# Hybrid decoder layer with a mixture of experts: pair 14's rows sent through memory, the residual rows loaded between the sent rows, two shared-row products moved

## The chip, the cores and the metric

The kernel runs on one core of one Trainium2 chip. The metric is the device time of one execution in microseconds, as the median of several runs; lower is better. Engines are named as in the profile: PE is TensorE, DVE VectorE, ACT ScalarE, POOL GpSimd, SP the SyncE that issues most DMAs.

## The reference

One decoder layer over 512 tokens of width 1024 (16 learned meta tokens in front). First a mixer (latent attention heads beside short convolutions), which ends in a residual sum `h`. Then the part that matters here:

```python
h = h + rms_norm(mix, post_mix_norm[l])
ffn = hier_moe(rms_norm(h, pre_ffn_norm[l]), ...)
h = h + rms_norm(ffn, post_ffn_norm[l])
```

`hier_moe` routes each token to one of 4 groups and to the best 2 of the group's 8 experts (32 experts in all, width 256), and adds one shared expert that every token goes through:

```python
hid = jax.nn.silu(a) * b * combine[:, :, None]
routed = jnp.einsum('nef,efd->nd', hid, w_down)
shared = (jax.nn.silu(t @ w_sh_gate) * (t @ w_sh_up)) @ w_sh_down
return (routed + shared).reshape(bsz, slen, d)
```

All data is float32.

## The kernel before, in words

The program is written out instruction by instruction. Generators (`pairs_gen`, `last_gen`, `shared_gen` and others) are spawned with priorities, and `run` picks at build time the one that can go on first by a model of the engines' progress; the order that results is fixed in the program. A `yield` names what the generator waits for in that model.

The 32 experts are taken as 16 pairs, j = 0 to 15 (`pairs`, line 393). An expert holds up to 64 tokens in the main path; a pair fills the 128 rows of a tile. For each pair `pairs_gen` (line 1452) does this: the pair's tokens are gathered from `t_d` in memory into `xg` by an indirect transfer on GpSimd, transposed into `wk` (`pxt`), multiplied with the two gate-and-up blocks of each expert (`pgu`, blocks `(e, 0)` and `(e, 1)`, 1 MB each), gated (`hidden`, ScalarE and VectorE), transposed again (`pht`), and multiplied with the down block `(e, 2)` in two halves (`pdn`).

What becomes of a pair's rows depends on `PE_PAIRS` (line 56), here 2, so `first` is 14. Pairs 0 to 13 copy the down product into `yb` (one half by ScalarE, one by VectorE) and `send` it: an indirect transfer on GpSimd writes each row to its place in `y_d`, whose 1024 rows hold two rows for each token. Pairs 14 and 15 go through TensorE: `y_out` splits the down product into a rounded part and a rest in `ys`, a selection matrix `sel` is built from the token numbers, and sel times `ys` puts the rows at their tokens. For pair 14 this is `combine`: sixteen products `pcb` between the two gate-and-up halves of pair 15, each pair of them added by VectorE to the shared expert's rows `sho` (`acc(c)`, four chunks of 128 tokens).

For pair 15 `last_gen` (line 1531) takes over. For each chunk c it collects two banks `pca` on TensorE: the shared rows times the identity (`inject`), `ys` times `sel`, and the sum of the two sent rows of each token times the identity (`ld kk`, loaded from `y_d` and added by VectorE in `rows`). Then ScalarE squares the banks for the norm, VectorE multiplies them by the gain (`tm`), GpSimd takes the power (`rf`), and `store` adds the residual `h` (`ld hb`, loaded from `h_d`) and issues the output. Before, chunks 0 and 1 are injected ahead of the last down product, chunks 2 and 3 in their turn. A last copy by ScalarE puts `pca` back into `acc(c)`, for the case that some expert holds more than 64 tokens: then a branch at the end (`overflow`) handles the rest. With these inputs the trace shows no work in that branch.

The weights and the last loads stand in one list, `Slots.queue`, in the order of the `queue_load` calls (lines 379 to 406). They go into 25 buffers of 1 MB each and are issued in that order on SP's queue. A DMA on SP waits for the semaphore of the DMA eight places ahead of it, and a `kk` load also for the sends into `y_d`. An instruction that waits on SP holds everything behind it.

Of the kernel before, what the change touches and what calls it, by code (L numbers as in the profile page):

```python
# [18 lines left out]
P = 128  # L19
D = 1024  # L20
NT = 4
# [31 lines left out]
LAT_TO_PE = 0.2  # L53
GROUPS = ((0, 2), (2, 4))
POOL_M = 4
PE_PAIRS = 2

# [106 lines left out]
def hymba_kernel(ctx: ExitStack, tc: tile.TileContext, xT, xmT, x, meta, cpk, pos, wqkv, wconv, wuq, wukv,  # L166
# [120 lines left out]
    def at(*aps):  # L287
        return lambda: max(PR.when(a) for a in aps)

    def free_bank(n=1):  # L290
        def f():
            if len(banks) + n <= NBANK:
                return 0.0
            return sorted(done(b) for b in banks)[len(banks) + n - NBANK - 1]
        return f
# [7 lines left out]
    def flag(d, *names):  # L303
        return lambda: 0.0 if all(n in d for n in names) else INF
# [4 lines left out]
    def every(*needs):  # L309
        return lambda: max(f() for f in needs)  # L310
# [64 lines left out]
    def queue_load(name, src, n=2048, ok=None):  # L375

        Slots.queue.append((name, src, n, ok))
# [22 lines left out]
        if j == S_AT:  # L400
            queue_load((NE, 2), we[NE, 2])
    queue_load("gp", g_post[None, :].to_broadcast([P, D]), D)
    for q in range(2):
        queue_load(f"hb{q}", h_d[q * 256:(q + 1) * 256, :].rearrange("(q p) d -> p q d", p=P))
    for c in range(NT):
        queue_load(f"kk{c}", y_d[:, :].rearrange("(k c p) d -> c p k d", k=2, c=NT)[c], ok=lambda: "sent" in cv)


    jp = m1.bitcast(I32)[:, 0:P]
# [973 lines left out]
    def overflow():  # L1383

        n = nc.values_load(ov["novf"][0:1, 0:1], min_val=0, max_val=16)  # L1385
        with tc.If(n > 0):
            with tc.For_i(0, n, 1) as i:
                overflow_tile(i)
            post_again()
# [62 lines left out]
    def pairs_gen():  # L1452
        wk_, yb, ys, box = rt["wk"], rt["yb"], None, None
        rt["jk"] = wk_.bitcast(BF)[:, 3584:3584 + 512]
        xt_ = wk_[:, :D]
        sg, hd, ht = (wk_[:, D + q * 256:D + (q + 1) * 256] for q in range(3))
        yield every(at(xg[0]), free_bank(2))
        xpose(xg[0], xt_)
        gather(2)
        first = NP - PE_PAIRS  # L1460
        for j, es in enumerate(pairs):
            ps = None
            for i in range(2):
                yield every(loaded(*((e, i) for e in es)), free_bank())
                w = [got((e, i)) for e in es]
                yield at(*w, xt_)
                if ps is None:
                    ps = bank("pgu")
                for k in range(4):
                    col2(ps, xt_[:, (4 * i + k) * P:(4 * i + k + 1) * P],  # L1470
                         [w[q][:, k * 512:(k + 1) * 512] for q in range(2)], i + k == 0, i + k == 4)
                rel(*w)
                if j > first and i == 0:
                    yield flag(sh, "done")
                    for half in range(2):
                        for c in range(NT):
                            yield every(at(ys), free_bank())
                            combine(ys, sel, HALF[half], c)
            hidden(ps, wgt[:, j:j + 1], sg, hd)
            sh["silu"] = True  # L1480
            if j == S_GO:
                sh["go"] = True
            if j == first:
                box = reserve("ys", dt=F32R)
                rel(yb)
                yield lambda: 0.0 if box else INF
                rt["ys"] = ys = box[0]
            if j + 1 < NP:
                yield every(at(xg[(j + 1) % 2]), free_bank(2))
                xpose(xg[(j + 1) % 2], xt_, V)  # L1490
            if j + 3 < NP:
                gather(j + 3)
            yield every(at(hd), free_bank())
            hidden_t(hd, ht)
            if j >= first:
                V.tensor_tensor(sel.rearrange("p (c n) -> p c n", c=NT), iop[:, None, :].to_broadcast([P, NT, P]),
                                tok[:, :, j:j + 1].to_broadcast([P, NT, P]), op=OP.is_equal)
            if j == NP - 1:
                spawn(last_gen(es), 5)
                return  # L1500
            yield every(loaded(*((e, 2) for e in es)), free_bank(2))
            w = [got((e, 2)) for e in es]
            yield at(*w, ht)
            for half in range(2):
                ps = down(half, ht, [t[:, half * D:(half + 1) * D] for t in w])
                if j >= first:
                    y_out(ps, ys, HALF[half])
                else:
                    o = yb[:, j % 2 * D:(j % 2 + 1) * D][:, HALF[half]]
                    if half:  # L1510
                        V.tensor_copy(o, ps)
                    else:
                        S.activation(o, ps, AF.Copy)
            rel(*w)
            if j < first:
                send(j, yb[:, j % 2 * D:(j % 2 + 1) * D])
            if j == first - 1:
                cv["sent"] = True
# [6 lines left out]
    def down(half, ht, w):  # L1525
# [2 lines left out]
            col2(ps, ht[:, f * P:(f + 1) * P], [w[q][:, f * 512:(f + 1) * 512] for q in range(2)], f == 0, f == 1)  # L1528
        return ps

    def last_gen(es):


        ys, ht = rt["ys"], rt["wk"][:, D + 512:D + 768]
        ss, rf = small([P, 2 * NT], "ssf"), small([P, NT], "rf")
        var = small([P, 2 * NT], "var")
        pa, kk = {}, {}

        def inject(c):

            for half in range(2):
                pa[c, half] = bank("pca")
                held.append(pa[c, half])
                mm(pa[c, half], ident, acc(c)[:, HALF[half]], start=True, stop=False)

        for c in range(2):
            yield every(flag(sh, "done"), at(acc(c)), free_bank(2))
            inject(c)
        yield every(loaded(*((e, 2) for e in es)), free_bank(2))
        w = [got((e, 2)) for e in es]  # L1550
        yield at(*w, ht)
        for half in range(2):
            y_out(down(half, ht, [t[:, half * D:(half + 1) * D] for t in w]), ys, HALF[half])
        rel(*w)
        tm = reserve("tm0", "tm1")
        yield every(loaded("gp", "hb0", "hb1"), lambda: 0.0 if len(tm) == 2 else INF)
        gp, hb = got("gp"), [got("hb0"), got("hb1")]
        fin.update(gp=gp, tm=tm)

        def rows(c):  # L1560

            kk[c] = got(f"kk{c}")
            V.tensor_tensor(kk[c][:, :D], kk[c][:, :D], kk[c][:, D:2 * D], op=OP.add)

        def tmc(c, o=slice(0, D)):
            return tm[c // 2][:, c % 2 * D:(c % 2 + 1) * D][:, o]

        def store(c):
            h = hb[c // 2][:, c % 2 * D:(c % 2 + 1) * D]
            for q in HALF:  # L1570
                V.scalar_tensor_tensor(h[:, q], tmc(c, q), rf[:, c:c + 1], h[:, q], op0=OP.mult, op1=OP.add)
                Y.dma_start(out[c * P:(c + 1) * P, q], h[:, q])

        yield loaded("kk0")
        rows(0)
        for c in range(NT):
            if c >= 2:
                yield free_bank(2)
                inject(c)
            yield at(ys)  # L1580
            for half in range(2):
                for q in range(2):
                    mm(pa[c, half], sel[:, c * P:(c + 1) * P], ys[:, q * D + half * 512:q * D + (half + 1) * 512],
                       start=False, stop=False)
            yield at(kk[c])
            for half in range(2):
                mm(pa[c, half], ident, kk[c][:, HALF[half]], start=False, stop=True)
            if c + 1 < NT:
                yield loaded(f"kk{c + 1}")
                rows(c + 1)  # L1590
            for half in range(2):
                S.activation(rt["jk"], pa[c, half], AF.Square, accum_out=ss[:, 2 * c + half:2 * c + half + 1])
                V.tensor_tensor(tmc(c, HALF[half]), pa[c, half], gp[:, HALF[half]], op=OP.mult)
            v = var[:, 2 * c:2 * c + 2]
            V.tensor_scalar(v[:, 0:1], ss[:, 2 * c:2 * c + 1], 1.0 / D, EPS, op0=OP.mult, op1=OP.add)
            V.scalar_tensor_tensor(v[:, 1:2], ss[:, 2 * c + 1:2 * c + 2], 1.0 / D, v[:, 0:1], op0=OP.mult, op1=OP.add)
            G.tensor_tensor(rf[:, c:c + 1], v[:, 1:2], neghalf[:, 0:1], op=OP.pow)
            for half in range(2):
                S.activation(acc(c)[:, HALF[half]], pa[c, half], AF.Copy)
                held.remove(pa[c, half])  # L1600
            if c:
                store(c - 1)
        store(NT - 1)

# [93 lines left out]
```

## Time and profile before

| | |
|---|---|
| median of 3 runs | 516.67 us (515.33 to 517.06) |
| the profiled execution | 516.31 us |
| its span, first to last instruction | 514.5 us |
| busy in the span: PE, DVE, ACT, POOL | 95%, 45%, 33%, 17% |
| moved by DMA | 151.07 MB, mean 294 GB/s |
| mean granted TensorE clock | 0.994 |

The page gives shares over the whole span. The change lies in the last 50 us or so, so the views of that stretch, engine by engine, say more: the instructions in order of time, the windows of 2 us, and the DMA issues with their time from issue to landing. A row of the order of time gives start, duration, engine, line, operation, tiles, how many, and in brackets the idle time before it and what ended it. A landing is the time at which the transfer's semaphore came, counted from its issue. Most instructions have line 314 or 159, those of two helpers; they are told apart by their tiles.

### The profile page before, as it was taken

The page shows a single profiled execution, that of the slowest core. Times are in us where ns is not written, and L with a number is a line of the kernel's source. Part 1 is how long each engine was busy: PE and PEld are TensorE (multiplying, and loading weights), DVE is VectorE, ACT ScalarE, POOL GpSimd, SP SyncE. Part 2 cuts the span into 40 slices and gives each one's busy share as a digit, 9 for nine tenths or more (in the row PEclk, how much of TensorE's full clock was granted, in tenths as well). Part 3 has the DMA queues.
Part 4 walks back from the last instruction along what each step waited for, and adds up shares of the span by engine and source line. Part 5 has one row for each costly group of instructions (what it writes and reads, how often), then busy time and mean ns, then how long its engine had stood idle before and what let it go on. Part 6 is the DMA issues. An engine that isn't in the chain of part 4 may idle for free. (4 is left out here: it accounts for less than half of the span.)

```text
span 514.5 us, 7298 instructions
## 1 busy us (share of the span) xinstructions
PE 487.5 (95%) x2782; PEld 306.5 (60%) x2782; DVE 232.9 (45%) x532; ACT 168.9 (33%) x343; POOL 88.0 (17%) x113
## 2 busy tenths in 40 slices
PE   7999999999999999999999999999999998889992
PEld 7998999788767788898844333433333332323341
DVE  6467789657878633588821200111111111003384
ACT  5775526444444642441211221211111111101152
POOL 2034234400000003540201110111111110000011
PEclk9999999999999999999999999999999999999997
DMA  8952240190208578499289999999999999999953
GB/s 288 400 236 82 83 164 0 46 365 0 83 25 300 211 304 329 172 384 395 88 347 392 425 420 421 422 418 422 417 421 418 420 419 419 423 420 421 408 214 125
DMA packets 30165, 151.07 MB, mean 294 GB/s; under 512 B 5392, under 2 KB 5776, under 8 KB 16048
## 3 DMA queue, kind: packets, MB, share of 16 engines
q1 hardware_dynamic: 24512, 138.43, 67.0%
q0 software_dynamic: 4320, 7.94, 4.2%
q10 hardware_dynamic: 1296, 4.21, 2.0%
q8 instruction: 23, 0.38, 0.3%
q14 instruction: 14, 0.11, 0.1%
HBM read 140.54 MB, written 17.83 MB: 308 GB/s over the span
## 5 line engine op out<-in xcount | busy, mean ns | idle before, releaser
L314 PE MATMUL pc<-xh,cw 128*128 128x256 f32 (+2 forms) x320 | 70.0, 309 | 0.0
L159 DVE SCALAR_TENSOR_TENSOR wk<-wk,wgt,pgu 128x256 f32<-128x256 f32 x16 | 7.7, 480 | 110.3 <-ACT wk L159 110.3
L314 PEld LDWEIGHTS pc<-xh,cw 128*128 128x128 f32 x320 | 52.3, 189 | 4.0 <-issue 1.3
L159 ACT ACTIVATE wk<-pgu 128x256 f32<-128x256 f32 x16 | 6.2, 384 | 142.0 <-PE pgu L314 142.0
L314 PE MATMUL pc<-xl,cw 128*128 128x256 f32 (+2 forms) x160 | 48.8, 305 | 0.0
L159 POOL DMA_INDIRECT xg<-t_d,idx x16 | 17.0, 1065 | 113.8 <-PE pxt L314 69.2
L159 DVE COPY yb<-pdn 128x512 f32<-128x512 f32 x14 | 9.7, 692 | 55.4 <-PE pdn L314 55.4
L314 PEld LDWEIGHTS pc<-xl,cw 128*128 128x128 f32 x160 | 30.3, 189 | 1.2
L159 POOL DMA_INDIRECT y_d<-yb,sidx x14 | 14.1, 1010 | 81.1 <-DVE yb L159 60.2
L159 ACT ACTIVATE att<-pS,nm 128x128 f32<-128x128 f32 (+3 forms) x32 | 16.9, 528 | 29.3 <-DVE nm L159 27.2
L314 PE MATMUL pS<-kT,qT 128*128 128x128 f32 (+3 forms) x64 | 22.7, 440 | 0.0
L159 POOL TENSOR_TENSOR sst<-rst,neghalf 128x1 f32<-128x1 f32 x12 | 7.6, 635 | 81.5 <-DVE rst L159 78.1
L314 PEld LDWEIGHTS pxt<-ident,xg 128*128 128x128 f32 x128 | 14.0, 141 | 11.3 <-issue 7.8
L314 PE MATMUL pco<-wo,cvh 128*128 128x512 f32 x64 | 20.6, 403 | 0.0
L314 PE MATMUL pao<-wo,mgh 128*128 128x512 f32 x64 | 20.0, 393 | 0.0
L159 POOL TENSOR_TENSOR cw<-ld conv,cw 128x1024 fp32r<-128x1024 f32 x6 | 15.7, 2625 | 18.5 <-ACT cw L159 18.5
L314 PE MATMUL psh<-tT,ld (32, 0)_1930 128*128 128x128 f32 x128 | 18.8, 280 | 0.0
L314 PE MATMUL psh<-tT,ld (32, 1)_1932 128*128 128x128 f32 x128 | 17.8, 277 | 0.0
L314 PE MATMUL pxt<-ident,xg 128*128 128x128 f32 x128 | 17.3, 278 | 0.0
L159 ACT ACTIVATE yb<-pdn 128x512 f32<-128x512 f32 x14 | 8.4, 597 | 26.0 <-PE pdn L314 26.0
L314 PEld LDWEIGHTS psh<-tT,ld (32, 0)_1930 128*128 128x128 f32 x128 | 16.2, 192 | 0.2 <-issue 0.2
L159 DVE TENSOR_REDUCE nm<-pS 128x1 f32<-128x128 f32 (+3 forms) x32 | 15.5, 484 | 1.7 <-PE pS L314 1.4
(490 smaller groups left out, 1214.6 us busy)
## 6 DMA issues: line engine op xcount, KB each, us to landing
ld conv<-in_wconv_dram SPq DMA_DIRECT2D x6, 1024.0 KB, 9.8
ld out<-in_wout_dram SPq DMA_DIRECT2D x4, 1024.0 KB, 5.1
y_d<-sel SPq DMA_DIRECT2D x4, 1024.0 KB, 7.2
ld kk<-y_d SPq DMA_DIRECT2D x4, 1024.0 KB, 19.0
xs<-in_x_dram SPq DMA_DIRECT2D x4, 512.0 KB, 9.1
x<-in_x_dram SPq DMA_DIRECT2D x4, 512.0 KB, 5.0
h_d<-mix ACTq DMA_DIRECT2D x4, 512.0 KB, 5.5
t_d<-x ACTq DMA_DIRECT2D x4, 512.0 KB, 6.7
```

The source lines that it names most:

```text
L159: r = f(*a, **k)
L314: f(o, *ins, **kw)
```

## The change

- `PE_PAIRS` becomes 1: pair 14 is copied into `yb` and sent like the pairs before it; only pair 15 goes through `ys` and `sel`. The sixteen `pcb` products and their eight additions leave the main path.
- `hb0` and `hb1` are queued behind `kk1` and `kk3`, not ahead of `kk0`; `store` waits for its own.
- `inject(0)` stands in `pairs_gen` ahead of pair 15's `pht`, `inject(1)` in `last_gen` behind the last down product.
- The copies of `pca` back into `acc(c)` are left out; the overflow branch now rebuilds these rows itself (combine and `kk` additions).

```diff
-PE_PAIRS = 2
+PE_PAIRS = 1
...
-    for q in range(2):
-        queue_load(f"hb{q}", h_d[q * 256:(q + 1) * 256, :].rearrange("(q p) d -> p q d", p=P))
     for c in range(NT):
         queue_load(f"kk{c}", y_d[:, :].rearrange("(k c p) d -> c p k d", k=2, c=NT)[c], ok=lambda: "sent" in cv)
+        if c % 2:
+            queue_load(f"hb{c // 2}", h_d[c // 2 * 256:(c // 2 + 1) * 256, :].rearrange("(q p) d -> p q d", p=P))
...
         with tc.If(n > 0):
+            for half in range(2):
+                for c in range(NT):
+                    combine(rt["ys"], sel, HALF[half], c)
+            for c in range(NT):
+                V.tensor_tensor(acc(c), acc(c), fin["kk"][c][:, :D], op=OP.add)
...
                 rel(*w)
-                if j > first and i == 0:
-                    yield flag(sh, "done")
-                    for half in range(2):
-                        for c in range(NT):
-                            yield every(at(ys), free_bank())
-                            combine(ys, sel, HALF[half], c)
             hidden(ps, wgt[:, j:j + 1], sg, hd)
...
+            if j == NP - 1:
+                yield every(flag(sh, "done"), free_bank(2))
+                inject(0)
             yield every(at(hd), free_bank())
             hidden_t(hd, ht)
...
-        for c in range(2):
-            yield every(flag(sh, "done"), at(acc(c)), free_bank(2))
-            inject(c)
...
         rel(*w)
+        yield free_bank(2)
+        inject(1)
         tm = reserve("tm0", "tm1")
-        yield every(loaded("gp", "hb0", "hb1"), lambda: 0.0 if len(tm) == 2 else INF)
+        yield every(loaded("gp"), lambda: 0.0 if len(tm) == 2 else INF)
...
             for half in range(2):
-                S.activation(acc(c)[:, HALF[half]], pa[c, half], AF.Copy)
                 held.remove(pa[c, half])
             if c:
+                yield loaded(f"hb{(c - 1) // 2}") if c % 2 else None
                 store(c - 1)
```

On TensorE, between the halves of pair 15's gate-and-up products (`ld (31, 0)` and `ld (15, 0)` are the first blocks, `ld (31, 1)` and `ld (15, 1)` the second):

```order
 L314 MATMUL pgu<-ld (31, 0)_3468,wk 64x512
 L314 MATMUL pgu<-ld (15, 0)_3470,wk 64x512
-L314 MATMUL pcb<-ys,sel 128x512 x16
 L314 MATMUL pgu<-ld (31, 1)_3484,wk 64x512
 L314 MATMUL pgu<-ld (15, 1)_3486,wk 64x512
```

The sixteen products of pair 14's combine are gone from here, and the second half follows the first.

On TensorE, behind that second half, around the transposes `pht` and the last down product `pdn` (`sho_2849` holds the shared rows of chunks 0 and 1):

```order
 L314 MATMUL pgu<-ld (15, 1)_3486,wk 64x512
+L314 MATMUL pca<-sho_2849,ident 128x512 x2
 L314 MATMUL pht<-ident,wk 128x128 x2
-L314 MATMUL pca<-sho_2849,ident 128x512 x4
 L314 MATMUL pdn<-ld (31, 2)_3496,wk 64x512
 L314 MATMUL pdn<-ld (15, 2)_3498,wk 64x512
@@ -1499,28 +1498,30 @@
 L314 MATMUL pdn<-ld (31, 2)_3496,wk 64x512
 L314 MATMUL pdn<-ld (15, 2)_3498,wk 64x512
+L314 MATMUL pca<-sho_2849,ident 128x512 x2
 L314 MATMUL pca<-ys,sel 128x512 x4
```

Of the four products with shared rows that stood between `pht` and `pdn`, chunk 0's two now stand ahead of `pht` and chunk 1's two behind `pdn`.

On SP, the loads behind the last weights, before:

```order
L159 DMA ld gp_3533<-in_g_post_dram 128x1024
L159 DMA ld hb0_3535<-h_d_72 128x2x1024
L159 DMA ld hb1_3549<-h_d_72 128x2x1024
L159 DMA ld kk0_3592<-y_d_73 128x2x1024
L159 DMA ld kk1_3594<-y_d_73 128x2x1024
L159 DMA ld kk2_3596<-y_d_73 128x2x1024
L159 DMA ld kk3_3598<-y_d_73 128x2x1024
```

and now:

```order
L159 DMA ld gp_3533<-in_g_post_dram 128x1024
L159 DMA ld kk0_3638<-y_d_73 128x2x1024
L159 DMA ld kk1_3640<-y_d_73 128x2x1024
L159 DMA ld hb0_3642<-h_d_72 128x2x1024
L159 DMA ld kk2_3644<-y_d_73 128x2x1024
L159 DMA ld kk3_3646<-y_d_73 128x2x1024
L159 DMA ld hb1_3648<-h_d_72 128x2x1024
```

`kk0`, which waits for the last send, now comes first, and the two `hb` loads, which wait for no send, stand behind it.

## Rows read from the trace of the kernel before

**Rows 1.** The page: span, and TensorE's granted clock in 40 slices.

```profile
span 514.5 us, 7298 instructions
...
PEclk9999999999999999999999999999999999999997
```

**Rows 2.** Windows: stretch, sum, five engines' busy time, PEclk, DMA share, GB/s.

```profile
484.00:486.00 2.00, 2.00 (x8) 0.60 (x8) 0.00 (x0) 0.00 (x0) 0.00 (x0) 1.00 1.03 410
...
510.00:512.00 2.00, 0.00 (x0) 0.00 (x0) 0.00 (x0) 0.00 (x0) 0.00 (x0) 0.50 0.60 224
```

**Rows 3.** TensorE in order of time, from pair 14's transposes to the end.

```profile
463.32 0.44 PE L314 MATMUL pht<-ident,wk 128*128 128x128 f32 x2
464.29 0.64 PE L314 MATMUL pdn<-ld (14, 2)_3431,wk 128*64 128x512 f32 x1 [0.53 <-ACT wk L159]
...
473.11 3.99 PE L314 MATMUL pcb<-ys,sel 128*128 128x512 f32 x16
477.04 0.64 PE L314 MATMUL pgu<-ld (31, 1)_3484,wk 128*64 128x512 f32 x1
...
481.69 0.44 PE L314 MATMUL pht<-ident,wk 128*128 128x128 f32 x2 [1.00 <-DVE wk L159]
481.96 3.60 PE L314 MATMUL pca<-sho,ident 128*128 128x512 f32 x8
485.49 0.64 PE L314 MATMUL pdn<-ld (31, 2)_3496,wk 128*64 128x512 f32 x1
...
489.08 1.27 PE L314 MATMUL pca<-ys,sel 128*128 128x512 f32 x3
...
491.70 1.98 PE L314 MATMUL pca<-ld kk,ident 128*128 128x512 f32 x4 [0.63 <-DVE ld kk L159]
...
498.81 1.88 PE L314 MATMUL pca<-ld kk,ident 128*128 128x512 f32 x4
...
503.18 1.88 PE L314 MATMUL pca<-ld kk,ident 128*128 128x512 f32 x4
```

**Rows 4.** VectorE in order of time: additions of sent rows, and the last chunk.

```profile
490.43 2.35 DVE L159 TENSOR_TENSOR ld kk<-ld kk 128x1024 f32<-128x1024 f32 x2
...
495.40 1.23 DVE L159 TENSOR_TENSOR ld kk<-ld kk 128x1024 f32<-128x1024 f32 x1
...
505.01 0.69 DVE L159 TENSOR_TENSOR tm<-pca,ld gp 128x512 f32<-128x512 f32 x1 [1.24 <-ACT wk L159]
```

**Rows 5.** SP's issues in order of time, then DMA issues: KB, us to landing.

```profile
453.74 0.33 SPq L159 DMA_DIRECT2D ld (15, 1)_3486<-in_we_dram  x1
...
458.70 0.33 SPq L159 DMA_DIRECT2D ld (15, 2)_3498<-in_we_dram  x1
461.71 0.33 SPq L159 DMA_DIRECT2D ld gp<-in_g_post_dram  x1
...
ld (15, 1)_3486<-in_we_dram SPq DMA_DIRECT2D x1, 1024.0 KB, 21.3
...
ld (15, 2)_3498<-in_we_dram SPq DMA_DIRECT2D x1, 1024.0 KB, 21.3
...
ld gp<-in_g_post_dram SPq DMA_DIRECT2D x1, 512.0 KB, 19.6
```

**Rows 6.** Pair 14's and 13's copies and send in time; the tile yb.

```profile
467.99 0.60 ACT L159 ACTIVATE ys<-pdn 128x512 fp32r<-128x512 f32 x1 [1.12 <-PE pdn L314]
...
454.01 0.99 POOL L159 DMA_INDIRECT y_d<-yb,sidx  x1 [14.97 <-DVE yb L159]
...
L159 DVE COPY yb<-pdn x14: 691/692/693, 268.5 to 452.5; 128x512 f32<-128x512 f32 x14
...
DMA to landing us min/median/max: 7.8/8.2/9.3
```

**Rows 7.** DMA queues from 456 to 464 us: pair 13's send (packets, MB, share).

```profile
q0 software_dynamic: 144, 0.24, 7.9%
```

**Rows 8.** TensorE's waits from 255 to 480 us: total, times, longest.

```profile
PE pgu L314 <- DMA ld (28, 1)_3291<-in_we_dram: 1.6, 1, 1.6
```

More of the change, by code (lines that the diff above doesn't have):

```diff
@@ L1529, in down, with inject @@
         return ps
+    pa = {}
+    def inject(c):
+        for half in range(2):
+            pa[c, half] = bank("pca")
+            held.append(pa[c, half])
+            mm(pa[c, half], ident, acc(c)[:, HALF[half]], start=True, stop=False)
     def last_gen(es):
@@ L1536, in last_gen @@
         var = small([P, 2 * NT], "var")
[L1537 to L1544, printed above, removed]
-        for c in range(2):
-            yield every(flag(sh, "done"), at(acc(c)), free_bank(2))
-            inject(c)
+        kk = {}
         yield every(loaded(*((e, 2) for e in es)), free_bank(2))
@@ L1554, in last_gen @@
         rel(*w)
+        yield free_bank(2)
+        inject(1)
         tm = reserve("tm0", "tm1")
-        yield every(loaded("gp", "hb0", "hb1"), lambda: 0.0 if len(tm) == 2 else INF)
-        gp, hb = got("gp"), [got("hb0"), got("hb1")]
-        fin.update(gp=gp, tm=tm)
+        yield every(loaded("gp"), lambda: 0.0 if len(tm) == 2 else INF)
+        gp, hb = got("gp"), {}
+        fin.update(gp=gp, tm=tm, kk=kk)
         def rows(c):
@@ L1568, in store @@
         def store(c):
+            if c % 2 == 0:
+                hb[c // 2] = got(f"hb{c // 2}")
             h = hb[c // 2][:, c % 2 * D:(c % 2 + 1) * D]
```

## The prediction

> **What bounds the kernel now.** I read the page first, then the windows, then the end of the program engine by engine. The profiled execution spans 514.5 us and took 516.31 us; the 1.8 us around the span stay. Towards the end the program is a stream of loads that keeps the DMA engines full: the window at 484 us shows them busy throughout, at 410 GB/s [rows 1, 2]. The change touches only what lies behind 466 us, so the question is what ends the program after the last weights.
>
> TensorE's order of time shows it [rows 3]. Pair 15's second half starts at 477.04, straight after the sixteen `pcb` products that combine pair 14 (473.11 to 477.04, 3.93 us). Its weights had landed: expert 15's second block was issued at 453.74 and took 21.3 us, so it was there at 475.04; the last down block, issued at 458.70, was there at 480.0, and `gp` (461.71 and 19.6) at 481.3 [rows 5]. Then comes 1.00 us of waiting for VectorE (before `pht`, 481.69), the transposes, four `pca` products that load shared rows of chunks 0 and 1 (481.96 to 485.49, 3.53 us), and only then the last down product, 5.5 us after its weights. From there TensorE runs almost without a gap to its last product, one chunk in 4.37 us (498.81 to 503.18). **So the end is set by TensorE's work behind pair 15's weights, not by the loads**, and a step taken out ahead of 491.70 moves the rest with it.
>
> **The change, part by part.**
>
> *The combine of pair 14 goes (16 `pcb`, 3.93 us).* Not all of it is won: the next product then waits for expert 15's second block at 475.04. The new send shares the DMA engines with that block. One send is 144 packets and 0.24 MB [rows 7], at 410 GB/s 0.6 us, so it delays the block by 0 to 0.6 us; pair 13's packets all lie between 456 and 464 us, 2 to 10 us behind its issue at 454.01 [rows 6, 7], and pair 14's send, issued at 469.5 (below), overlaps the block's last microseconds only in part. I take 0.3 and 0.1 to wake: the start goes from 477.04 to 475.4. The eight VectorE additions behind the combine go too; VectorE had nothing else there, so they are worth nothing.
>
> TensorE now waits between 473.1 and 475.4 where it worked. The first product of the other expert still runs in between, so the gap is about 1.8 us. The longest wait of this kind in the pairs before is 1.6 us (expert 28's second block), and the granted clock reads 9 in every slice but the last [rows 1, 8]; I charge nothing for it. [...]
>
> *Two of the four `pca` products move ahead of `pht`, two behind the last down product.* Two of them take half of 3.53, 1.77 us. Second half of pair 15 (477.04 to 480.69, that is 481.69 less the 1.00 wait): 3.65 us, now ending at 479.05. Chunk 0's two products follow, to 480.8; VectorE's hidden rows are there 1.00 us after 479.05, so that wait is filled and hidden. From `pht` to the first `pdn` pair 14 needed 0.97 us (463.32 to 464.29) [rows 3]. **The last down product starts at 481.8 instead of 485.49: 3.7 us earlier.** Its weights, at 480.0 plus at most 0.6, are there with 1.2 us to spare; were that cover gone, each later microsecond would count in full.
>
> Behind it, before: 6.21 us from the first `pdn` to the first `kk` product (485.49 to 491.70), ended by VectorE, which splits `ys` and then adds `kk0` (start 490.43, 1.2 us, so ready 6.2 us after the first `pdn`) [rows 3, 4]. Now TensorE needs 3.6 for the down product, 1.77 for chunk 1's shared rows and 1.0 for four `ys` products (sixteen took 3.93): 6.3 us. So 0.1 us is given back, and the `kk` products start at 488.1, **3.6 us earlier**.
>
> *Pair 14 is sent.* ScalarE's copy of the second half of pair 14's down product starts at 467.99; in pair 13 the issue on GpSimd followed 1.5 us after VectorE's copy of that half (452.5 and 454.01) [rows 6]. The issue is at 469.5; the fourteen sends before landed 7.8 to 9.3 us after theirs, median 8.2, so this one lands at 477.7, by 478.8 at worst. GpSimd's next work is the first chunk's power, behind the first `kk` products.
>
> *The loads on SP.* `kk0` waits for that send, where before only pair 13's send (issued at 454.01) stood ahead of it and it went out while the weights were still coming; everything on SP behind it (`kk1`, `hb0`, `kk2`, `kk3`, `hb1`) waits too. At 477.8 the weights to 480.0 and `gp` at 481.3 are still on their way, so the DMA engines have 3.5 us of work, and a load of 1 MB takes 2.56 us at 410 GB/s. If nothing runs dry, `gp` lands at 481.9 with the send's 0.6 us, and then one load each 2.56 us: `kk0` 484.4, `kk1` 487.0, `hb0` 489.6, `kk2` 492.1, `kk3` 494.7, `hb1` 497.2. VectorE wants them at its times before [rows 4] less 3.6: `kk0` and `kk1` at 486.8 and 488.0, `kk2` at 491.8 (495.40 before), `kk3` nearly a chunk later, the two `hb` later still. Only `kk2` is late, by 0.3 us, and VectorE has slack: 1.24 us idle in the last chunk, where it waits for ScalarE. Cost 0. Bounds: nothing if the loads come sooner, and 1.5 us if the DMA engines run dry for 2.5 us (2.8 us late less the slack of 1.24).
>
> *The rest.* ScalarE loses eight copies of `pca` back into the shared rows. They stand behind the squares of their chunk and VectorE's products; TensorE's chunks follow each other without waiting for them: 0. The longer branch for overflowing experts is not entered: 0.
>
> **Sum.** 516.31 − 3.7 + 0.1 = 512.7 us against the profiled execution. That one lies 0.36 us below the median of the runs, so the forecast is 513.1. The ends: the block undelayed and TensorE quicker to wake give 0.4 more (512.7); the late loads at their bound give 1.5 back (514.6).
>
> **Rivals.**
>
> 1. *Part of it is given back.* The late loads above at their bound, or the send delaying both the second block and the last down block by more than its bytes, 1 to 2 us: 514.0 to 515.4. For it: the weights' 21 us in the queue show how deep it is. Against: fourteen sends went through the same stream, and TensorE's waits for weights stayed at 1.6 us and below [rows 8]. Chance 0.15, four fifths of it still over 0.3% faster.
>
> 2. *The loads starve, and it is slower.* Place: SP, which stands at `kk0` until the send lands. While it stands nothing new enters the queue; the work on its way lasts until 481.3, and from then on every microsecond of the send's landing shifts all six loads. VectorE's slack, less the 0.3 us already used, takes 0.9 us. So a landing at 482 costs nothing yet, at 486 it costs 3.6 us and the gain is gone (516.7), and from 487.3, that is 18 us after its issue, the kernel is slower by over 0.3% (518.2 and more). The way from an issue to its first packet, which no row here shows apart, brings these points forward by its length. For it: the wait is new, and it stands ahead of everything else on SP. Against: 9.3 us is the longest of fourteen landings [rows 6]. Chance 0.05, 0.03 of it slower.
>
> 3. *The clock falls in the new gap.* At the lower level (granted clock 0.50 in the last window of rows 2, after TensorE had been done for several microseconds) work takes twice as long: the 3.65 us of pair 15's second half would cost 3.65 more, and the gain would be gone (516.7); lasting through the down product (1.77 + 1.0 + 3.6 more), 522. [...] Against: rows 1 and 8. Chance 0.03.
>
> 4. *No effect that can be measured*, because VectorE and not TensorE sets the pace of the last chunks and starts them no earlier: 516 to 517. Against: VectorE's 1.24 us of waiting in the last chunk, and that its first `kk` addition hangs on the last down product too [rows 4]. Chance 0.05.
>
> **How the numbers follow.** The forecast, 512.2 to 514.0, has 0.72. Two runs of this kernel can't be told apart within about 0.3%, 1.55 us: faster means below 515.1, slower above 518.2. Faster: 0.72 and 0.12 of rival 1, 0.84. Same: the rest of rival 1 (0.03), 0.02 of rival 2, 0.02 of rival 3, rival 4: 0.12. Slower: 0.03 and 0.01: 0.04. The range runs from 511.6 (the best ends of the terms and 0.2% of scatter, as the runs before show) to 515.6, which takes in rival 1; rivals 2 to 4, 0.13, stay outside.
>
> **What would show it.** The second half of pair 15 starts at about 475.4 and waits for expert 15's second block; `pdn` starts near 482 directly behind `pht`; `kk0` is issued near 478 after a wait for the send; the first `kk` product is near 488, and the chunks still take 4.4 us each; the DMA engines stay full until about 495. Wrong would be: a hole in the DMA engines' rate around 480, TensorE or VectorE waiting for `kk` or `hb` by more than a microsecond, `pdn` waiting for weights, or a granted clock below 1.00 before 500.

## The result, and the profile after

The changed kernel takes **510.06 us** (median of 4 runs, 509.64 to 510.31) against 516.45 us (4 runs, 515.33 to 517.06) for the kernel before on the same chip: ratio 0.9881, 95% interval 0.9869 to 0.9893. That is 6.4 us, where 3.6 were forecast; the time lies 1.5 us below the forecast's range. The profiled execution took 509.86 us.

The page of the kernel after, against [rows 1]:

```profile
span 508.1 us, 7246 instructions
...
PEclk9999999999999999999999999999999999999998
```

Its windows, against [rows 2] (stretch, sum, five engines' busy time, PEclk, DMA share, GB/s):

```profile
472.00:474.00 2.00, 0.70 (x4) 0.20 (x4) 0.00 (x0) 0.00 (x0) 0.00 (x0) 1.00 0.99 406
474.00:476.00 2.00, 2.00 (x12) 0.65 (x9) 0.00 (x0) 0.00 (x0) 0.00 (x0) 1.00 1.02 420
476.00:478.00 2.00, 2.00 (x8) 0.66 (x5) 0.18 (x1) 0.38 (x1) 0.00 (x0) 1.00 0.89 367
478.00:480.00 2.00, 1.50 (x5) 0.50 (x4) 0.90 (x2) 0.39 (x1) 0.00 (x0) 1.00 0.91 313
480.00:482.00 2.00, 1.97 (x10) 0.77 (x12) 0.00 (x0) 0.00 (x0) 0.00 (x0) 1.00 1.01 412
```

The clock stays at its upper level, through TensorE's idle time between 472 and 474 us too. While SP waits for the send, the DMA rate dips for 4 us and is back at 412 GB/s at 480.

TensorE in order of time, against [rows 3]:

```profile
473.72 0.64 PE L314 MATMUL pgu<-ld (15, 1)_3486,wk 128*64 128x512 f32 x1 [1.30 <-DMA ld (15, 1)_3486<-in_we_dram]
...
477.30 1.98 PE L314 MATMUL pca<-sho,ident 128*128 128x512 f32 x4
479.12 0.38 PE L314 MATMUL pht<-ident,wk 128*128 128x128 f32 x2
480.03 0.64 PE L314 MATMUL pdn<-ld (31, 2)_3496,wk 128*64 128x512 f32 x1 [0.53 <-ACT wk L159]
...
483.62 1.99 PE L314 MATMUL pca<-sho,ident 128*128 128x512 f32 x4
485.04 1.48 PE L314 MATMUL pca<-ys,sel 128*128 128x512 f32 x4
486.36 1.88 PE L314 MATMUL pca<-ld kk,ident 128*128 128x512 f32 x4
...
497.76 1.88 PE L314 MATMUL pca<-ld kk,ident 128*128 128x512 f32 x4
```

The wait that the prediction asked for is there, 1.30 us for expert 15's second block; then TensorE's order is the one forecast, only earlier. VectorE, against [rows 4], and then GpSimd, against [rows 6]:

```profile
484.97 2.35 DVE L159 TENSOR_TENSOR ld kk<-ld kk 128x1024 f32<-128x1024 f32 x2
...
490.81 1.23 DVE L159 TENSOR_TENSOR ld kk<-ld kk 128x1024 f32<-128x1024 f32 x1 [0.81 <-DMA ld kk<-y_d]
...
499.60 0.69 DVE L159 TENSOR_TENSOR tm<-pca,ld gp 128x512 f32<-128x512 f32 x1 [0.82 <-ACT wk L159]
```

```profile
469.11 0.98 POOL L159 DMA_INDIRECT y_d<-yb,sidx  x1 [14.43 <-DVE yb L159]
```

`kk2` is the late load, 0.81 us, and no product of TensorE waits for it. SP's issues in order of time, then the landings (KB, us), against [rows 5]:

```profile
453.41 0.33 SPq L159 DMA_DIRECT2D ld (15, 1)_3486<-in_we_dram  x1
...
477.24 0.90 SPq L159 DMA_DIRECT2D ld kk<-y_d  x2
478.24 0.42 SPq L159 DMA_DIRECT2D ld hb<-h_d  x1
```

```profile
ld (15, 0)_3470<-in_we_dram SPq DMA_DIRECT2D x1, 1024.0 KB, 20.3
ld (31, 1)_3484<-in_we_dram SPq DMA_DIRECT2D x1, 1024.0 KB, 20.3
ld (15, 1)_3486<-in_we_dram SPq DMA_DIRECT2D x1, 1024.0 KB, 20.3
ld (31, 2)_3496<-in_we_dram SPq DMA_DIRECT2D x1, 1024.0 KB, 20.9
ld (15, 2)_3498<-in_we_dram SPq DMA_DIRECT2D x1, 1024.0 KB, 20.9
```

In the kernel before, the load ahead of expert 15's second block took 0.5 us less than the block itself:

```profile
ld (31, 1)_3484<-in_we_dram SPq DMA_DIRECT2D x1, 1024.0 KB, 20.7
```

The send lands 8.1 us after its issue and frees SP at 477.24. Expert 15's second block needs 20.3 us instead of 21.3. The send's packets come too late to touch it: the DMA queues of the kernel after from 472 to 474 and from 474 to 476 us (packets, MB, share) show

```profile
q0 software_dynamic: 34, 0.06, 7.6%
```

```profile
q0 software_dynamic: 90, 0.16, 20.9%
```

The first of the 144 packets starts at 473.28, when the block is 0.4 us from its landing, and the last at 476.55. It is the down blocks behind it that land later, 20.9 us after their issue.

The span's 6.4 us by stretches, each from the rows above and those of before:

| stretch | before | after | gain | forecast |
|---|---|---|---|---|
| up to the issue of (15, 1) | 453.74 | 453.41 | 0.33 | 0 |
| from it to the start of pair 15's second half | 23.30 | 20.31 | 2.99 | 1.64 |
| from there to the first `kk` product | 14.66 | 12.64 | 2.02 | 1.96 |
| first to last `kk` product | 11.48 | 11.40 | 0.08 | 0 |
| last `kk` product to the end ("tail") | 11.32 | 10.34 | 0.98 | 0 |

So two stretches hold the miss: the landing of the block, and the tail, which the change does not touch. From the last `kk` product to VectorE's last instruction both kernels take 6.3 us (503.18 to 509.48, and 497.76 to 504.06); what differs is the stores behind it. "DMA to landing" of the eight stores, first of before and then of after:

```profile
DMA to landing us min/median/max: 2.0/2.5/3.0
```

```profile
DMA to landing us min/median/max: 2.0/2.2/2.5
```

### The profile page after: what moved, and what is told of

It is laid out like the page before. It is cut to its first block, busy times and chain, and to the rows that moved or that the text cites. A ratio compares the mean times of both kernels' runs of the same rounds, so it can differ in the third digit from the quotient of the medians.

```text
span 508.1 us, 7246 instructions
## 1 busy us (share of the span) xinstructions
PE 481.9 (95%) x2766; PEld 304.0 (60%) x2766; DVE 226.6 (45%) x522; ACT 164.0 (32%) x334; POOL 88.0 (17%) x114
## 5 line engine op out<-in xcount | busy, mean ns | idle before, releaser
L159 DVE COPY yb<-pdn 128x512 f32<-128x512 f32 x15 | 10.4, 692 | 59.3 <-PE pdn L314 59.3
L314 PEld LDWEIGHTS pxt<-ident,xg 128*128 128x128 f32 x128 | 14.0, 141 | 11.3 <-issue 7.8
```

The costliest lines, as they stand in the source:

```text
L159: r = f(*a, **k)
L314: f(o, *ins, **kw)
```

## Experiments

"Block" is expert 15's second block, its landing counted from its issue. A "fetch" is a packet of an instruction queue (q8 or q14) among the DMA packets. The letters of the theories are those of the expectations.

**The kernel before once more** (no edit).

> The kernel before, unchanged, profiled a second time. Theory A (the loads that SP queues behind the weights make the weights land later): expert 15's second block again takes about 21.3 us from issue to landing, 3.0 us after the block ahead of it, where the changed kernel shows 20.3 and 2.5. Theory B (that difference is scatter from run to run): 20.3 to 20.9 and 2.5. The last store: about 3.0 us from issue to landing if its lateness belongs to the program, about 2.0 if it is scatter. Time 515.3 to 517.1.

516.78 us; block 21.5, tail 515.1 − 503.90 = 11.2 us. Both of before's long stretches come again, so they are no accident of one profile.

**Without pair 14's send.**

```diff
-            if j < first:
+            if j < first - 1:
                 send(j,
```

> The changed kernel without pair 14's send: those rows are missing from the output, and the first load of sent rows no longer waits for that send, so SP issues it and what follows at about 464 instead of 477. Theory A: these loads then stand behind the weights again and delay them: expert 15's second block lands about 1 us later (21.3 us from its issue), pair 15's second half starts at about 474.7 instead of 473.7, and the kernel is slower by about 1 us, 511 us, although it does less. Theory B: the block lands as in the changed kernel or 0.3 us sooner (no send beside it), start 473.4 to 473.7, time 509.7 to 510.1.

511.54 us (510.89 to 512.59), ratio 0.9919 [0.9897, 0.9941]: *less* work, and 1.5 us slower than the first runs with the send (0.8 us slower than the slowest of the changed kernel's three medians, e17). SP issues the loads from 463 us on, as before; block 21.2, tail 509.2 − 497.81 = 11.4. This seemed to bear out theory A: loads queued behind the weights hold the weights and the stores up.

**`hb` ahead of `kk` as before.**

```diff
+    for q in range(2):
+        queue_load(f"hb{q}", ...)
     for c in range(NT):
         queue_load(f"kk{c}", ...)
-        if c % 2:
-            queue_load(f"hb{c // 2}", ...)
```

> The changed kernel with the two h loads queued ahead of the sent rows again, as before. Both theories: the first load of sent rows still goes out at about 477 but now stands behind 2 MB, so it lands near 488 instead of 483 and the first product with sent rows starts at about 490 instead of 486.4: 3 to 4.5 us slower, 513 to 514.5 us. Theory A adds: the two h loads go out at 464 and 466.6, expert 15's first or second block lands 0.4 to 1 us later than in the changed kernel, so pair 15's second half starts at 474.1 to 474.7; theory B: at 473.7. The prediction's own step (order of the loads costs nothing): 510.1.

515.35 us (514.0 to 516.93), ratio 0.9987 [0.9974, 1.0000]. TensorE in order of time:

```profile
486.00 1.50 PE L314 MATMUL pca<-ys,sel 128*128 128x512 f32 x4
490.36 1.98 PE L314 MATMUL pca<-ld kk,ident 128*128 128x512 f32 x4 [2.87 <-DVE ld kk L159]
```

and VectorE:

```profile
489.08 1.22 DVE L159 TENSOR_TENSOR ld kk<-ld kk 128x1024 f32<-128x1024 f32 x1 [3.07 <-DMA ld kk<-y_d]
```

The order of the loads is not an ornament: without it the wait for `kk0` gives back nearly the whole gain. Tail 512.3 − 501.83 = 10.5. The profile is of the fastest of ten runs and 4.1 us longer than the changed kernel's (514.0 against 509.86); the medians differ by 5.3. Two of the ten runs took 514.0 and 514.2 us at a mean granted clock of 0.997, the other eight 515.0 to 516.9 us at 0.990 to 0.993. So behind the wait of 2.87 us TensorE's clock probably fell in most runs; no trace of such a run was kept.

**The shared rows' products where they were.**

```diff
-            if j == NP - 1:
...
-                inject(0)
...
+        for c in range(2):
...
+            inject(c)
         yield every(loaded(*((e, 2) for e in es)), free_bank(2))
...
-        inject(1)
```

> The changed kernel with all four products of the shared rows of chunks 0 and 1 between the transposes and the last down product, as before. By the prediction's steps: the last down product starts 2.0 us later (1.00 us waiting for VectorE, 3.53 of products instead of 1.77), and 0.1 comes back behind it: 512.0 us. Rival (the down product waits for its weights or VectorE anyway, so the place is worth nothing): 510.1.

512.66 us (512.36 to 514.0), ratio 0.9940 [0.9917, 0.9964]. From the start of pair 15's second half to the first `kk` product 489.14 − 474.49 = 14.65 us, as before; the term is 2.0 us, as forecast. Tail 10.4.

**The changed kernel again** (no edit).

> The changed kernel once more, for a second profile. Theory A (loads of h and of the sent rows that stand in SP's queue behind the weights make the weights land about 1 us later and leave the last stores about 1 us slower; the changed kernel, whose SP waits for the send until 477 us, escapes both): 509.6 to 510.6 us, expert 15's second block lands 20.3 to 20.8 us after its issue, from the start of the last kk product to the end of the span 10.3 to 10.5 us. Theory B (landing and tail of the first profile were a lucky draw): the landing is 21 to 21.5 us or the tail 11 us or more, and the time is 511 to 512.5 us.

510.5 us (509.41 to 510.94), ratio 0.9882 [0.9865, 0.9899]; block 20.7, tail 509.1 − 498.77 = 10.3.

**The kernel before, its loads held back.**

```diff
-        queue_load(f"hb{q}", ...)
+        queue_load(f"hb{q}", ..., ok=lambda: "hold" in cv)
...
                             combine(ys, sel, HALF[half], c)
+                            if half == 1 and c == 0:
+                                Y.dma_start(scr, acc(0)[0:1, 512:1024])
+                                cv["hold"] = True
```

> The kernel before, whose SP waits at a transfer of one row of 2 KB, ready when chunk 0's second half is combined (about 475 us), before it queues h and the sent rows. TensorE combines until 477 us as before, so a weight that lands sooner changes nothing there. Theory A: expert 15's second block lands 20.3 to 20.8 us after its issue instead of 21.3 to 21.5; h and the sent rows land between 483.6 and 496.4 us, in time for VectorE (kk0 wanted at 490.4); the tail behind the last kk product is 10.3 to 10.5 us instead of 11.2, so 515.5 us. Theory B: landing and tail vary by chance, 516.4 us. A rival for the tail (it hangs on how the sent rows are read, not on the hold): landing 20.3 to 20.8, tail 11.2, 516.4 us.

516.14 us (515.01 to 517.93), ratio 1.0008 [0.9996, 1.0020]; block 20.9, tail 513.2 − 502.13 = 11.1. The tail does not hang on the hold; the block lies between what the theories asked for.

**No send, loads held to 478 us, and to 469 us.**

```diff
             hidden(ps, wgt[:, j:j + 1], sg, hd)
...
+            if j == NP - 1:
+                Y.dma_start(scr[:, :256], sg[0:1, :])
+                cv["sent"] = True
...
-            if j < first:
+            if j < first - 1:
                 send(j,
...
-                cv["sent"] = True
```

> The changed kernel without pair 14's send (pair 14's rows are left out of the result), SP held at a transfer of 1 KB that is ready at about 478 us, so that the other loads start as late as in the changed kernel. Without the hold, without the send, it was 511.5 us, block landing 21.2, tail 11.4 us. Theory A (the hold is what helps): 509.3 to 510.4 us, landing 20.3 to 20.8, tail 10.3 to 10.5 us. Theory C (the hold has no part in it): 511.0 to 511.8 us, landing 21 or more, tail 11 or more.

511.4 us (510.94 to 512.1), ratio 0.9909 [0.9892, 0.9925]; block 20.7, tail 509.4 − 498.11 = 11.3. The second kernel took the row from `yb` instead, and its loads start at 468 us:

> The same with the hold ending at about 469 us, when pair 14's output is ready, some 4 us ahead of the landing of expert 15's second block. Theory A, if a queued load costs the weights in proportion to the time it stands in the queue: landing 20.6 to 21.0 us after its issue, 510.3 to 511.2 us. If only loads queued ahead of 469 us matter: as with the hold to 478 us, 509.3 to 510.4 us; if any queued load brings the whole cost: 511.0 to 511.8 us.

510.62 us in one run; block 20.7, tail 11.2. The hold buys no time that can be told from none, so theory A falls for the tail. What the six profiles with a tail of 11 us (before, e1, e2, e6, e7, e8) have in common is something else: none of these kernels sends pair 14.

The send itself has landed some 20 us ahead of these stores. But the trace shows the fetches of instructions among the DMA queues (q8 and q14), and there the two groups differ. DMA queues of the kernel before from 505 to 511 us, among the stores:

```profile
q14 instruction: 1, 0.01, 0.4%
```

The changed kernel has no such row between 498.7 and 505.9 us; its fetches on q14 start at 489.7 and at 506.6 us, and its last store has landed at 506.15. This is theory D: one more send is more instructions for GpSimd, and its next 8 KB are fetched at another time.

**Idle instructions on GpSimd, in the kernel before.**

```diff
                 cv["sent"] = True
+                for _ in range(8):
+                    G.memset(idl, 0.0)
```

> The kernel before with eight memsets of one column on GpSimd behind pair 13's send, where GpSimd has nothing else to do. Theory D (the extra 0.9 us behind the last kk product is one 8 KB fetch of GpSimd's instructions that lands among the last stores and holds up one DMA engine; the send of pair 14 adds instructions to GpSimd, so the same fetch comes some 30 us sooner and meets no store): the fetch at about 509 us goes to before 490 us, from the start of the last kk product to the end of the span 10.3 to 10.5 us instead of 11.2 to 11.3, the last store lands after 2.0 to 2.2 us, time 515.3 to 515.6 us against 516.3. Rival E (the shorter tail comes from the sent rows or from the order of the loads): tail 11.2 us, 516.3 us, no difference.

515.03 us (514.61 to 516.1, 10 runs) against 516.34 us, ratio 0.9977 [0.9968, 0.9987]. Eight instructions that do nothing make the kernel 1.2 us faster by this ratio, of which the tail shows 0.9. No q14 row is left among the stores, and they land sooner; the stores of this run:

```profile
DMA to landing us min/median/max: 2.0/2.1/2.1
```

Tail 512.9 − 502.44 = 10.5; block still 21.5. Theory D holds; E, by which the tail hangs on the sent rows or the order of the loads, is out.

**The same eight in place of pair 14's send.**

> The changed kernel without pair 14's send (its rows are left out of the result), with eight memsets of one column on GpSimd in place of the send. Without the memsets it was 511.5 us, the landing of expert 15's second block 21.2 us after its issue, the tail 11.4 us. Theory D: tail 10.3 to 10.5 us, 510.5 to 510.8 us, landing still about 21.2. Theory E: 511.5 us, tail 11.4.

510.33 us (509.75 to 511.56), ratio 0.9887 [0.9870, 0.9904]: 1.2 us less than without them, tail 508.0 − 497.56 = 10.4. The stores without the eight, then with them:

```profile
DMA to landing us min/median/max: 2.1/2.7/3.0
```

```profile
DMA to landing us min/median/max: 2.1/2.2/2.5
```

One part missed: the block landed after 20.3 us, not 21.2, although `kk0` and `kk1` stood in the queue from 463.6 us on. So theory A falls for the landing too. Nor is the send what makes the block land sooner: without it the block lands after 21.2 us (e2), 20.7 (e7, e8) and 20.3.

**The combine back.**

```diff
-PE_PAIRS = 1
+PE_PAIRS = 2
...
+                if j > first and i == 0:
+                    yield flag(sh, "done")
...
```

> The changed kernel with pair 14 combined by TensorE again and not sent; the order of the loads and the place of the shared rows' products stay as changed. By the prediction's terms (1.6 us for the start of pair 15's second half, nothing else): 510.1 + 1.6 = 511.7 us. By theories A and D together (the loads stand behind the weights again, the second half then starts straight behind the combine, 4.0 + 3.9 us behind the start of expert 15's first block, that is about 3.0 us later than in the changed kernel; and the fetch is back among the stores, 0.9): 513.5 to 514.1 us. With the landing alone, the tail as in the changed kernel: 513.1 us.

514.57 us (514.16 to 515.42), ratio 0.9966 [0.9953, 0.9979]. The second half starts at 477.33, 23.5 us behind the block's issue, and the tail is 512.7 − 501.37 = 11.3: the two stretches that the prediction missed, back together, and none of the others. Block 21.6. The time lies 0.5 us above what theories A and D asked for; in the profile 0.4 us of that is scatter ahead of the block's issue (453.81 against 453.41).

**ScalarE's copies back.**

```diff
             for half in range(2):
+                S.activation(acc(c)[:, HALF[half]], pa[c, half], AF.Copy)
                 held.remove(pa[c, half])
```

> The changed kernel with ScalarE's eight copies of pca back into the shared rows put back, behind the squares of each chunk. The prediction's term: 0, so 510.1 to 510.5 us. A rival: VectorE's last products wait for ScalarE (its idle time of 0.8 us in the last chunk ends there), so a copy of about 0.6 us a half that ScalarE does ahead of the next chunk's squares costs up to 1.2 us: 511.5 us.

511.4 us (510.7 to 512.43), ratio 0.9906 [0.9890, 0.9922], which overlaps that of every run of the changed kernel. By the time alone the rival (511.5) would do as well. The profile speaks against it: the stretches behind the block are the changed kernel's, 12.64, 11.38 and 10.4 us, and what comes later is the block's issue, by 0.67 us (454.08), ahead of any copy. The term is 0 within what can be told.

**Idle instructions on VectorE, ScalarE and GpSimd, in the changed kernel.** Left was the landing. Both kernels fetch 8 KB at 472.6 us; the changed one fetches once more at 489.7. Theory F: a fetch sets one DMA engine back, and a load lands with its slowest engine; so it matters which engine's instructions come when. Sixteen (eight on GpSimd) idle instructions stand where `cv["sent"]` is set; on VectorE:

```diff
                 cv["sent"] = True
+                for _ in range(16):
+                    V.memset(idl, 0.0)
```

> The changed kernel with sixteen memsets of one column on VectorE at about 469 us, where it has nothing to do until 477 us. Theory F (the 8 KB fetch at 472.6 us in the kernel before, at 489.7 us in the changed one, sets one DMA engine back, and a load lands with its slowest engine): if that fetch is VectorE's, it comes at 469 to 473 us now, expert 15's second block lands 20.9 to 21.4 us after its issue instead of 20.3 to 20.8, 510.7 to 511.2 us. If it is another engine's, or F is wrong: 510.1 to 510.5 us, landing 20.3 to 20.8.

510.78 us (510.42 to 511.64), ratio 0.9892 [0.9875, 0.9908]. The fetch is VectorE's: it comes at 467.0 us now and is gone at 489. Landings of this run:

```profile
ld (31, 0)_3469<-in_we_dram SPq DMA_DIRECT2D x1, 1024.0 KB, 20.2
ld (15, 0)_3471<-in_we_dram SPq DMA_DIRECT2D x1, 1024.0 KB, 20.8
...
ld (15, 2)_3499<-in_we_dram SPq DMA_DIRECT2D x1, 1024.0 KB, 21.3
```

The first load to land behind it (469.1 us) is 0.6 us later than the one ahead, and what follows stays late; the send's packets then add 0.5 us to (31, 2) and (15, 2). The block lands after 20.8 us: just under the 20.9 to 21.4 that theory F asked for, and at the top of the 20.3 to 20.8 of its rival. The time can't be told from the changed kernel's. What speaks for F is the place at which the delay comes in, which moved with the fetch.

On ScalarE:

> The changed kernel with sixteen copies of one column on ScalarE at about 469 us, where it has nothing to do until 477 us. Theory F: if the fetch at 489.7 us is ScalarE's, it comes at 469 to 473 us now, expert 15's second block lands 20.9 to 21.4 us after its issue, 510.7 to 511.2 us. If it is another engine's, or F is wrong: 510.1 to 510.5 us, landing 20.3 to 20.8.

510.07 us (509.64 to 510.62), ratio 0.9875 [0.9859, 0.9892]; the fetch at 489 stays, block 20.5. ScalarE's is another, at 466.8 here and 469.7 us in the changed kernel.

On GpSimd:

> The changed kernel with eight memsets of one column on GpSimd behind pair 13's send. Its fetch, at 472.6 us in the changed kernel, comes at another time ahead of 472 us; the tail stays at 10.3 to 10.5 us, the landing at 20.3 to 20.8, 510.1 to 510.5 us. If idle instructions on GpSimd help by themselves and not by the fetch: 509.0 to 509.5 us.

510.52 us (509.76 to 510.67), ratio 0.9878 [0.9861, 0.9894]; block 20.9, tail 10.4. In this kernel `cv["sent"]` is set behind pair 14's send, not pair 13's, and GpSimd's fetch stayed where it was, at 472.5 us, not earlier as expected. Where the fetch stays, idle instructions gain nothing.

**Chunk 0's products into the wait for the block.**

```diff
             for i in range(2):
+                if j == NP - 1 and i == 1:
...
+                    inject(0)
                 yield every(loaded(*((e, i) for e in es)), free_bank())
...
-            if j == NP - 1:
...
-                inject(0)
```

> The changed kernel with chunk 0's two shared-row products between the first and the second half of pair 15, into TensorE's wait for expert 15's second block, instead of behind the second half. If the landing of that block sets the start: the second half starts at most 0.5 us later behind the issue of the block (1.8 of work against 1.3 of wait), the wait for VectorE ahead of pht (1.0 us) is back, the product behind it needs no 1.8 any more: pht 0.3 us earlier behind the landing, 0.3 us less in all, 509.9 us against 510.2. If the start hangs on something else, the products come on top: 1.3 to 1.8 us more at the start, 1.0 more in all, 511.2 us.

> The changed kernel a third time, beside e16: 509.8 to 510.6 us, expert 15's second block lands 20.3 to 20.9 us after its issue, tail 10.3 to 10.5 us.

e16 takes 510.32 us (509.63 to 510.88), ratio 0.9896 [0.9879, 0.9912], beside 510.73 us (509.98 to 511.35), ratio 0.9904 [0.9888, 0.9921], for the changed kernel. The profiles say the same more finely: from the block's issue to the first `kk` product 32.81 us (453.33 to 486.14) against 32.97 (453.52 to 486.49). The 1.8 us of products move the second half's start by 0.55 us only (20.87 us behind the block's issue instead of 20.32), so the landing of the block does set the start. What is won is too little to tell it from the changed kernel in time.

## Why the prediction was wrong

The sign and the chain were right; two terms of the sum were mis-sized.

- **"The start goes from 477.04 to 475.4"** is the step that failed first: 473.72, 1.35 us sooner behind the block's issue. It took the block's landing as fixed at 475.04, added 0.3 us for the send and 0.1 to wake. The send's packets come with the block's last 0.4 us and cost it nothing that can be seen, and the wake is 0.04 us; the other 1.0 us is the landing itself. The changed kernel's block takes 20.3, 20.7 and 20.3 us in its three profiles, that of the kernels that combine pair 14 and queue their loads freely 21.3, 21.5, 21.5 and 21.6 in four (before, e1, e9, e11). Part of this is shown. VectorE's fetch comes at 472 to 473 us in those four, and the block lands 0.5 to 0.6 us later behind its issue than the load ahead of it. (That this fetch is VectorE's there too is inferred: with the combine put back, e11, the one at 489.7 is gone and one at 473.0 is there.) In e6 the fetch came at 477.3, and the load late by 0.6 us was the one that landed behind that, (15, 2). In e13 it was put at 467.0, and (15, 0) was the late one. The change takes away the combine's additions on VectorE, and its next fetch moves to 489.7 us, behind the weights. The remaining 0.3 to 0.5 us is not settled. Between the first two profiles it is 0.4 us and enters with the load that lands behind ScalarE's fetch at 467 to 470 us, which cost between 0 and 0.6 us from run to run; in e1, e9 and e11 0.2 to 0.3 us is there already at (31, 0), ahead of these fetches. I know no rule for either.
- **"The 1.8 us around the span stay", and with them everything behind the last product,** is the other. The sum had no term for the tail, as the change has no instruction there. It measured 0.98 us: GpSimd's fetch among the stores, which the send's instructions move away (e9, e10 and e11 move it in and out).
- *The combine as work hidden behind a landing:* right. TensorE waits for the block (1.30 us), and e16 shows that the wait is real slack.
- *Shared rows' products, 2.0 us:* right (2.02; e4 14.65 against 12.64).
- *`pdn` directly behind `pht`, its weights there:* right; `pdn` waits 0.53 us for ScalarE alone. *6.3 us to the `kk` product:* 6.33.
- *Send and loads:* issue forecast 469.5, was 469.11; landing 477.7, was 477.2; `kk2` late by 0.3 forecast, 0.81 measured, and hidden as argued. The 0.6 us that the send's bytes might cost shows, but on the down blocks: with the send (31, 2) lands 0.5 to 0.7 us later behind its issue than the load ahead of it (after, e3, e4, e5, e12), without it as the load ahead (e2, e7, e8, e10). `pdn` waits for ScalarE and not for them, with 0.8 us to spare (479.26 to 480.03) where 1.2 were forecast. "Cost 0" was right for the new order alone: e3 prices the old one at 4.1 us in its profile.
- *Copies 0:* right within what can be told.
- **Rivals.** 1 (given back): did not come. 2 (starving): the windows show its beginning, 367 and 313 GB/s, and it ended at 480 because the send landed in 8.1 us. 3 (the clock): 1.00 in every window shown, behind a gap of 1.30 us. The Trainium skill, "TensorE: Matmul & The Clock Gate", section "Why this matters for your kernels", warns of a fall of the clock behind longer gaps than this one; the trace agrees, and the nearest to such a fall are the slower runs of e3. 4: refuted.
- **The sum.** 1.35 of the landing, 0.98 of the tail, 0.33 of scatter ahead of the change and 0.14 of small terms are the 2.8 us between 3.6 and 6.4. The changed kernel's medians in its three sets of runs are 510.06, 510.5 and 510.73 us, so some of the first comparison's gain was luck, about 0.4 us; with it or without it the time lies below the range.

## What to carry to other kernels

A landing read from a trace is not a constant of the load: it holds whatever else the DMA engines did in those 20 us, so its scatter over runs belongs into the range, on the good side too. Where a kernel ends on a few small stores, look in the DMA queues for a fetch of instructions among them; any change in an engine's number of instructions can move it in or out, and a result within 0.3% should be tested against a few idle instructions before it is put down to the edit. And price the whole of a reordering: the order of the loads cost nothing as it was, and 4 to 5 us when undone.

## What the runs showed of the hardware

- **One 8 KB fetch of instructions cost the kernel 1.2 us** (0.9977 [0.9968, 0.9987], 0.9 of it seen in the tail), when it fell among the last 256 KB stores: those near it landed after 2.9 to 3.0 us instead of 2.0 to 2.1. Its own packet took only 0.34 us (0.4% of 16 engines' time from 505 to 511); how it costs the stores more than that is not shown. The Trainium skill, "Runtime: NRT & Kernel Launch", section "Instruction fetch mechanics", calls the cost of going from one block of instructions to the next mostly hidden; in the tail of this kernel it was not hidden from the stores.
- **A load lands with the slowest of its DMA engines.** The trace has sixteen landing records for each load. In the kernel before those of (31, 1) are spread over 2.31 us and those of the block, behind the fetch, over 2.85; the spread then stays, 2.86 and 2.87 for the next two loads. In the changed kernel the spread is 2.86 for (15, 0) already and the fetch at 472.6 us (by exclusion GpSimd's; e2, without the send, has none there) does not widen it: 2.86 for the block. It is 3.51 for (31, 2), amid the send's packets, and 3.01 again for (15, 2). So not every fetch costs a load something. That this one set back an engine which was not the last fits, but the profile does not tell which engine a packet ran on.
- **Loads queued behind others did not delay them:** block 20.3 us with 2 MB queued 7 to 10 us ahead of its landing (e10), 20.7 us with none (e7).
- **Behind a send of 0.23 MB the loads land 0.5 to 0.7 us later.** Its 144 packets start 4.2 us behind the issue on GpSimd (469.11 to 473.28) and take 0.61 us of all 16 engines, so the delay is about the send's own time. GpSimd's fetch at 472 to 473 us comes in the same kernels; what part it has is not told apart.
